# The final norm written with features on partitions instead of token rows

## The chip, the cores and the metric

The kernel runs on one core of one Trainium2 chip, in one launch. The metric is the time of an execution on the device in microseconds (us), of which the median of three runs is given.

## The reference, cut to what matters

One layer of a hybrid decoder and a final norm, all in float32, for 512 prompt tokens and 8 sample tokens of 1024 features. A recurrent mixer comes first; the part around the change is the MLP and the final norm:

```
h2 = rmsnorm(x, norm2_g) * (1 + sc2) + sh2
ff = square(relu(h2 @ w_ff1)) @ w_ff2          # 1024 -> 4096 -> 1024
x  = x + g2 * ff                               # g2: one row for the prompt, one per sample
y  = x * rsqrt(mean(x * x over features) + 1e-6) * final_norm_g
```

The outputs are y for the prompt and for the samples, and the states of the mixer.

## The kernel before, in words

All tokens stand side by side in one axis of T = 520 (512 prompt, 8 samples), cut into two halves of HALF = 260. Activations lie with features on partitions: `self.x` is a list of 8 tiles of 128 features x 520 tokens, called features or feature blocks 0 to 7 here. A float32 product is made of three matmuls with operands split into a high and a low part (`_split_w`, L107: the high part by a ScalarE cast, the low part by a VectorE subtraction).

The MLP (`mlp`, L1351) goes in four quarters q of the 4096 hidden features. In each, the second matrix is multiplied by a Strassen-like scheme: for each pair m of output blocks (2m and 2m + 1) there are seven products, named by j, of 12 matmuls over 260 columns each (`product`, L1180). Each product accumulates in a PSUM bank that it shares with others of its pair, and after each, `added` (L1303) reads the bank and adds what belongs to x: by VectorE directly, or by a ScalarE copy (`snap`, L1212) and an accumulating DMA from POOL. The eight sample columns are collected in `zs` and added at the pair's end. The order of the products is written out in `plan` (L1028); the last quarter ends with (2,1), (2,2), (2,6), (2,7), (3,1), (2,4), (3,6), (3,2), (3,7), (2,5), (3,4), (2,3), (3,5), (3,3), where (m,j) is pair and product. For m = 2, block 4 is complete in its first half after (2,2), (2,4) completes the first half of block 5, (2,5) its second, and (2,3) the second half of block 4. For m = 3 (`added_last`, L1447), block 6's first half is complete after (3,2), block 7's after (3,4), and the second halves after (3,5) for block 7 and (3,3) for block 6.

The framework's planner orders each engine's instructions by a simulated timeline; `urgent` raises a priority, and `InOrder` (L53) fixes the written order on TensorE, ScalarE and VectorE. From (3,4)'s result on everything is in the written order.

The final norm before writes y in token rows. `final_pair` (L1419) transposes two feature blocks of half the tokens on TensorE against the identity, sums squares over them on ScalarE, and multiplies by the norm's weights on VectorE (`gbc`, a row loaded by L1400 and spread over all partitions) into `fx`, 4 x 128 token rows of 1024 features; the samples go to `fxs`. Blocks 6 and 7 come last: `last_transposes` (L1543) multiplies by a diagonal of the norm's weights instead, and `last_sums` (L1550) adds their squares on TensorE to those collected. `last_half` (L1521), behind (2,3), makes the roots of the first 256 tokens and writes their rows, the part behind (3,3) the rest; `row` (L1566) multiplies 128 rows by their roots, one scalar per partition, in a piece of 768 and one of 256 features, and sends each off. Rows leave in runs of 3072 and 1024 bytes.

Of the kernel before, what the change touches and what calls it, by code (L numbers as in the profile page):

```python
# [6 lines left out]
F32 = mybir.dt.float32  # L7
# [4 lines left out]
OP = mybir.AluOpType  # L12
# [5 lines left out]
NB = 8  # L18
# [23 lines left out]
NM = 9  # L42
T2 = T + NM + 3
# [36 lines left out]
class Kernel:  # L80
# [188 lines left out]
    def load_parameters(self):  # L269
# [4 lines left out]
        self.gcol = self.pm[:, 70:72]  # L274
# [905 lines left out]
    def product(self, q, m, j, ks):  # L1180
# [13 lines left out]
        for k in ks:  # L1194
# [7 lines left out]
            if (q, m, j, k) == (3, 2, 3, 2):  # L1202
                self.last_rows = [self.ppb.tile([128, 512], F32, name="pb"), self.ppt.tile([128, 512], F32, name="pt")]
                self.last_transposes(0, 0)
                self.last_transposes(0, 1)
# [97 lines left out]
    def added(self, q, m, j, ps, s):  # L1303
# [35 lines left out]
        if j == 3:  # L1339
# [3 lines left out]
            if q == 3:  # L1343
                eng = nc.gpsimd if far else nc.vector
                for t in (0, 1):
                    eng.tensor_tensor(zs[t], zs[t], self.modc(5, 2 * m + t)[:, 1:9], OP.mult)
                    eng.tensor_tensor(x[t][:, L:], x[t][:, L:], zs[t], OP.add)
# [46 lines left out]
    def final_open(self):  # L1394
        nc, sm = self.nc, self.consts
        self.fx = self.act.tile([128, NC, D], F32, tag="h", name="fx", bufs=2)
        t = self.act.tile([128, 4, D], F32, tag="h", name="fin", bufs=2)
        self.gbc, self.fxs, self.junk = t[:, 0], t[:NB, 1], t[:, 2].rearrange("p (n f) -> p n f", f=256)
        self.njunk = 0
        nc.sync.dma_start(self.gbc, self.i["final_norm_g"].partition_broadcast(128))  # L1400
        self.fss = sm.tile([128, NC + 1, 4], F32, name="fss")
        nc.vector.memset(self.fss, 1.0)
        self.fr = sm.tile([128, 8], F32, name="fr")
        self.part = t[:, 3, 256:264]

# [680 lines left out]
```

## Time and profile before

| | us |
|---|---|
| median of three runs | 1005.66 (1005.57 to 1006.06) |
| the profiled execution | 1004.99 |
| its span, first to last instruction | 1003.2 |
| TensorE busy | 984.8 |
| VectorE busy | 690.4 |
| ScalarE busy | 524.3 |
| GpSimd (POOL) busy | 135.9 |

The span is what the trace covers; 1.8 us of the execution lie around it. The granted TensorE clock is 0.999 of full speed over the span. In the profile PE is TensorE, PEld its weight loads, DVE VectorE, ACT ScalarE, POOL GpSimd, SP the engine that issues most transfers; a q behind an engine's name is its sequencer. Instructions made through `InOrder` all carry line 72, so there the tile names tell them apart: `ma` is x, `snap` a copied product or a square, `fin` the final norm's tile, `mm`, `ps`, `pt` and `pb` are PSUM banks. A float32 matmul that is not split by hand appears as two instructions. The rows below are whole lines of the trace's views.

### The profile page before, as it was taken

The page shows a single profiled execution, that of the slowest core. Times are in us where ns is not written, and L with a number is a line of the kernel's source. Part 1 is how long each engine was busy: PE and PEld are TensorE (multiplying, and loading weights), DVE is VectorE, ACT ScalarE, POOL GpSimd, SP SyncE. Part 2 cuts the span into 40 slices and gives each one's busy share as a digit, 9 for nine tenths or more (in the row PEclk, how much of TensorE's full clock was granted, in tenths as well). Part 3 has the DMA queues.
Part 4 walks back from the last instruction along what each step waited for, and adds up shares of the span by engine and source line. Part 5 has one row for each costly group of instructions (what it writes and reads, how often), then busy time and mean ns, then how long its engine had stood idle before and what let it go on. Part 6 is the DMA issues. An engine that isn't in the chain of part 4 may idle for free. (4 is left out here: it accounts for less than half of the span.)

```text
span 1003.2 us, 23199 instructions
## 1 busy us (share of the span) xinstructions
PE 984.8 (98%) x9644; PEld 955.0 (95%) x9644; DVE 690.4 (69%) x1359; ACT 524.3 (52%) x996; POOL 135.9 (14%) x247
## 2 busy tenths in 40 slices
PE   8999999999999999999999999999999999999997
PEld 6899999999989999989999999999999999999996
DVE  7795966676595667887535456767767766768785
ACT  5565645734653572475412234466556545646662
POOL 1300000000000101121000000022321331232050
PEclk9999999999999999999999999999999999999999
DMA  9663343243244336345557665222752472272142
GB/s 350 241 193 123 103 156 123 86 143 130 98 135 152 101 98 213 112 148 179 199 169 276 221 218 194 85 85 56 175 153 80 104 194 83 64 189 65 64 85 86
DMA packets 48857, 143.67 MB, mean 143 GB/s; under 512 B 6240, under 2 KB 15904, under 8 KB 47720
## 3 DMA queue, kind: packets, MB, share of 16 engines
q1 hardware_dynamic: 37280, 123.47, 36.4%
q0 software_dynamic: 11456, 18.70, 8.3%
q8 instruction: 75, 1.23, 0.5%
q14 instruction: 30, 0.25, 0.1%
q10 hardware_dynamic: 16, 0.03, 0.0%
HBM read 123.65 MB, written 11.26 MB: 134 GB/s over the span
## 5 line engine op out<-in xcount | busy, mean ns | idle before, releaser
L155 PE MATMUL mm<-h,whi 128*128 128x260 f32 (+1 forms) x2720 | 451.4, 285 | 0.0
L155 PEld LDWEIGHTS mm<-h,whi 128*128 128x128 f32 x2720 | 378.3, 188 | 1.3 <-issue 0.6
L155 PE MATMUL mm<-h,wlo 128*128 128x260 f32 x1360 | 279.9, 285 | 2.6 <-DVE wlo L116 2.6
L116 DVE TENSOR_TENSOR wlo<-wst,whi 128x1024 fp32r<-128x1024 f32 x156 | 190.7, 1224 | 126.0 <-ACT whi L113 121.8
L113 ACT CAST whi<-wst 128x1024 fp32r<-128x1024 f32 x156 | 163.8, 1052 | 187.8 <-PE mm L155 142.1
L155 PEld LDWEIGHTS mm<-h,wlo 128*128 128x128 f32 x1360 | 212.4, 189 | 3.9 <-DVE wlo L116 3.2
L1293 POOL TENSOR_TENSOR ft<-ft,fsh 128x8 f32<-128x8 f32 x28 | 18.4, 659 | 209.2 <-DVE ft L1287 209.2
L1301 DVE TENSOR_TENSOR f<-f 128x260 f32<-128x260 f32 x64 | 27.3, 427 | 28.0 <-ACT f L1296 27.5
L1290 ACT ACTIVATE ft<-ft,fsh 128x512 f32<-128x512 f32 (+2 forms) x36 | 24.1, 677 | 36.0 <-DVE ft L1287 36.0
L155 PE MATMUL mm<-b,whi 128*128 128x260 f32 x256 | 41.6, 284 | 0.0
L155 PE MATMUL mm<-oa,whi 128*128 128x260 f32 x256 | 41.6, 284 | 0.0
L155 PE MATMUL mm<-a,whi 128*128 128x260 f32 x256 | 41.4, 284 | 0.0
L582 DVE TENSOR_TENSOR X<-X,tb 128x512 f32<-128x512 f32 x48 | 31.0, 690 | 12.5 <-PE ps L574 9.2
L155 PEld LDWEIGHTS mm<-oa,whi 128*128 128x128 f32 x256 | 34.8, 188 | 2.1 <-ACT whi L113 1.6
L155 PEld LDWEIGHTS mm<-b,whi 128*128 128x128 f32 x256 | 35.1, 188 | 1.7 <-ACT whi L113 1.2
L155 PEld LDWEIGHTS mm<-a,whi 128*128 128x128 f32 x256 | 35.0, 188 | 1.2 <-PE pt L359 0.8
L231 POOL TENSOR_SCALAR ss<-ss 128x4 f32<-128x4 f32 x8 | 2.7, 334 | 238.2 <-ACT g L666 238.1
L179 ACT ACTIVATE gate<-pb,pa 128x260 f32<-128x260 f32 x32 | 15.5, 485 | 31.1 <-PE pb L714 31.1
L1335 POOL DMA_DIRECT2D ma<-snap x28 | 26.2, 951 | 40.5 <-issue 28.7
L1317 POOL DMA_DIRECT2D ma<-snap x28 | 26.0, 929 | 37.8 <-DMA ma<-snap 22.4
L1296 ACT ACTIVATE f<-ft 128x520 f32<-128x520 f32 (+1 forms) x36 | 20.8, 589 | 15.1 <-POOL ft L1294 13.1
L155 PE MATMUL mm<-b,wlo 128*128 128x260 f32 x128 | 25.8, 283 | 0.0
(566 smaller groups left out, 2072.7 us busy)
## 6 DMA issues: line engine op xcount, KB each, us to landing
wst<-in_w_ff_dram SPq DMA_DIRECT2D x64, 512.0 KB, 4.1
wst<-in_w_in_dram SPq DMA_DIRECT2D x56, 512.0 KB, 3.7
wst<-in_w_mod_dram SPq DMA_DIRECT2D x32, 512.0 KB, 4.3
wm<-in_w_piece_dram SPq DMA_DIRECT2D x4, 1024.0 KB
wm<-in_w_rows_dram SPq DMA_DIRECT2D x4, 1024.0 KB, 12.1
st<-in_state_hgrn_dram SPq DMA_DIRECT2D x8, 512.0 KB, 3.8
vb<-vd SPq DMA_DIRECT2D x8, 512.0 KB, 4.0
out_dram<-st SPq DMA_DIRECT2D x8, 512.0 KB
```

Source lines behind the costliest of these rows:

```text
L113: ins = self.nc.scalar.copy(hi, st)
L116: self.nc.vector.tensor_tensor(lo, st, hi.bitcast(F32), OP.subtract)
L155: self.last_product = self.nc.tensor.matmul(ps[s][:, :c.stop - c.start], x, y[:, c], start=first and n == 0, stop=last and n == 2)
L179: ins = self.nc.scalar.activation(out, x, AF.Sigmoid, **kw)
L231: p.tensor_scalar(out, x, n * EPS, None, OP.add)
L582: last = nc.vector.tensor_tensor(half, half, factors(tbs, x, b), OP.mult)
L1290: nc.scalar.activation(t[:, :p], t[:, :p], AF.Relu, bias=sh[:, 0:1])
L1293: eng.tensor_tensor(t[:, p:], t[:, p:], sh[:, 1:9], OP.add)
L1296: nc.scalar.activation(f, self.two(self.ft)[:, a:a + n], AF.Square)
L1301: self.nc.vector.tensor_tensor(f[:, n], f[:, a], f[:, b], op)
L1317: nc.gpsimd.dma_start(x[1][:, b], v[:, :n], accum_op=OP.add)
L1335: nc.gpsimd.dma_start(x[t][:, a], s[p], accum_op=OP.add)
```

## The change

The result stays with features on partitions. Its output is one array of 8 x 128 x 520, features by tokens, which is only laid out anew outside the kernel. No block of x is transposed any more and the row of norm weights isn't loaded.

For each block, `final_in` squares it on ScalarE, makes `xg`, the block times the norm's weights (one scalar per partition, `gcol`), by a ScalarE Copy, and adds the square to `total` on VectorE. When a half of all blocks is in, `final_roots` sums `total` over partitions on TensorE, in three groups of 87 tokens (matmuls of one column with `total` as weights), and takes the root on ScalarE; `final_diagonals` inverts it and makes three 87 x 87 diagonals on VectorE; `final_spread` multiplies them by ones, so that a PSUM bank holds each token's factor on all partitions; and `final_out` multiplies blocks a to b of half s by that bank on VectorE and sends them off, in runs of 260 tokens (1040 bytes). The first half's sums and diagonals come behind (2,3), its spread behind (3,5); all multiplies come behind (3,3), where block 6's second half takes weights and factor in one instruction. The sample columns of the odd blocks are now finished after j = 5, those of the even ones after j = 3.

```diff
--- before.py
+++ after.py
@@ -40,6 +40,7 @@
 
 
 NM = 9
+GROUP = 87
 T2 = T + NM + 3
 PAIR = "pair"
 EARLY = 8
@@ -271,7 +272,7 @@
         self.pm = self.consts.tile([128, 72], F32, name="pm")
         self.nc.sync.dma_start(self.pm, self.i["params_mod"])
         self.bmod, self.n1g, self.n2g = self.pm[:, 0:48], self.pm[:, 48:56], self.pm[:, 56:64]
-        self.gcol = self.pm[:, 70:72]
+        self.gcol = self.pm[:, 64:72]
         self.pl = self.start.tile([128, 16], F32, name="pl")
         self.nc.sync.dma_start(self.pl, self.i["params_bound"])
         self.pa = t = self.hc.tile([128, 313], F32, name="pa")
@@ -1199,10 +1200,6 @@
                                             stop=k == 3 and n == 2, skip_group_check=True)
                 self.behind(ins, self.last_product)
                 self.last_product = ins
-            if (q, m, j, k) == (3, 2, 3, 2):
-                self.last_rows = [self.ppb.tile([128, 512], F32, name="pb"), self.ppt.tile([128, 512], F32, name="pt")]
-                self.last_transposes(0, 0)
-                self.last_transposes(0, 1)
         if ks[-1] == 3:
             if (q, m) == (3, 3):
                 self.added_last(j, ps)
@@ -1340,11 +1337,10 @@
             with self.urgent():
                 nc.vector.scalar_tensor_tensor(x[0][:, b], ps[:, :n], g[0], x[0][:, b], OP.mult, OP.add)
                 nc.vector.tensor_tensor(zs[0], zs[0], ps[:, n:], OP.add)
-            if q == 3:
-                eng = nc.gpsimd if far else nc.vector
-                for t in (0, 1):
-                    eng.tensor_tensor(zs[t], zs[t], self.modc(5, 2 * m + t)[:, 1:9], OP.mult)
-                    eng.tensor_tensor(x[t][:, L:], x[t][:, L:], zs[t], OP.add)
+        if q == 3 and j in (5, 3):
+            t, eng = int(j == 5), nc.gpsimd if far else nc.vector
+            eng.tensor_tensor(zs[t], zs[t], self.modc(5, 2 * m + t)[:, 1:9], OP.mult)
+            eng.tensor_tensor(x[t][:, L:], x[t][:, L:], zs[t], OP.add)
         if q == 3:
             self.final_after(m, j)
 
@@ -1392,57 +1388,79 @@
         self.load()
 
     def final_open(self):
-        nc, sm = self.nc, self.consts
-        self.fx = self.act.tile([128, NC, D], F32, tag="h", name="fx", bufs=2)
-        t = self.act.tile([128, 4, D], F32, tag="h", name="fin", bufs=2)
-        self.gbc, self.fxs, self.junk = t[:, 0], t[:NB, 1], t[:, 2].rearrange("p (n f) -> p n f", f=256)
-        self.njunk = 0
-        nc.sync.dma_start(self.gbc, self.i["final_norm_g"].partition_broadcast(128))
-        self.fss = sm.tile([128, NC + 1, 4], F32, name="fss")
-        nc.vector.memset(self.fss, 1.0)
-        self.fr = sm.tile([128, 8], F32, name="fr")
-        self.part = t[:, 3, 256:264]
-
-        self.gdiag = t[:, 3, :256].rearrange("p (j f) -> p j f", j=2)
-        self.one, self.summed = self.ones_r.bitcast(F32)[:, 0:1], set()
+        t = self.act.tile([128, KO * T2], F32, tag="h", name="xg", bufs=2)
+        self.xg = t[:, :KO * T].rearrange("p (s m n) -> p s m n", s=2, m=KO)
+        t = self.act.tile([128, KO, T2], F32, tag="h", name="fin", bufs=2)
+        self.total, self.fsq, self.nsq = t[:, 0, :T], [t[:, 1 + n, :T] for n in range(5)], 0
+        self.diag = [t[:GROUP, 6 + s, :3 * GROUP].rearrange("p (i n) -> p i n", i=3) for s in range(2)]
+        self.fr = self.consts.tile([128, 8], F32, name="fr")
+
+    def final_in(self, t, *halves):
+
+        nc, x = self.nc, self.x[t]
+        c = slice(halves[0] * HALF, (halves[-1] + 1) * HALF)
+        if t:
+            self.nsq = (self.nsq + 1) % 5
+        sq = (self.fsq[self.nsq] if t else self.total)[:, c]
+        nc.scalar.activation(sq, x[:, c], AF.Square)
+        if (t, halves) != (6, (1,)):
+            nc.scalar.activation(self.xg[:, halves[0]:halves[-1] + 1, t], self.two(x)[:, halves[0]:halves[-1] + 1], AF.Copy,
+                                 scale=self.gcol[:, t:t + 1])
+        if t:
+            return lambda: nc.vector.tensor_tensor(self.total[:, c], self.total[:, c], sq, OP.add)
 
     def final_after(self, m, j):
         if (m, j) in ((2, 2), (2, 7)):
-            self.final_pair(int(j == 7), 0)
-            self.final_pair(int(j == 7), 1)
-        if (m, j) == (2, 7):
-            for t in range(2):
-                self.nc.vector.tensor_scalar(self.gdiag[:, t], self.ident, self.gcol[:, t:t + 1], None, OP.mult)
+            for t in (0, 1) if j == 2 else (2, 3):
+                add = self.final_in(t, 0, 1)
+                if add:
+                    add()
+        if (m, j) == (2, 4):
+            for t in (4, 5):
+                self.final_in(t, 0)()
+        if (m, j) == (2, 5):
+            self.final_in(5, 1)()
         if (m, j) == (2, 3):
-            self.last_half()
-
...
+            with self.urgent():
+                self.fsum, self.frs = (self.pmm.tile([128, 2, 512], F32, name="mm") for _ in range(2))
+                add = self.final_in(4, 1)
+                self.final_roots(0)
+                add()
+                self.final_diagonals(0)
+
+    def final_groups(self, s):
+        return [s * HALF + c for c in (0, GROUP, HALF - GROUP)]
+
+    def final_sums(self, s):
+        for n, c in enumerate(self.final_groups(s)):
+            self.nc.tensor.matmul(self.fsum[:GROUP, s, n:n + 1], self.total[:, c:c + GROUP],
+                                  self.ones_r.bitcast(F32)[:, 0:1], start=True, stop=True)
+
+    def final_roots(self, s):
+        self.final_sums(s)
+        r = self.fr[:GROUP, 4 * s:4 * s + 3]
+        self.nc.scalar.activation(r, self.fsum[:GROUP, s, :3], AF.Sqrt, bias=self.epsc[:GROUP], scale=1.0 / D)
+
+    def final_diagonals(self, s):
+        r = self.fr[:GROUP, 4 * s:4 * s + 3]
+        self.nc.vector.reciprocal(r, r)
+        self.nc.vector.tensor_tensor(self.diag[s], self.ident[:GROUP, None, :GROUP].to_broadcast([GROUP, 3, GROUP]),
+                                     r[:, :, None].to_broadcast([GROUP, 3, GROUP]), OP.mult)
+
+    def final_spread(self, s):
+        for n, c in enumerate(self.final_groups(0)):
+            self.nc.tensor.matmul(self.frs[:, s, c:c + GROUP], self.ones_r.bitcast(F32)[:GROUP], self.diag[s][:, n],
+                                  start=True, stop=True)
+
+    def final_out(self, s, a, b):
+
+        y, r = self.xg[:, s, a:b], self.frs[:, s, :HALF]
+        if (s, a) == (1, 6):
+            self.nc.vector.scalar_tensor_tensor(y[:, 0], self.x[6][:, HALF:], self.gcol[:, 6:7], r, OP.mult, OP.mult)
+        else:
+            self.nc.vector.tensor_tensor(y, y, r[:, None].to_broadcast([128, b - a, HALF]), OP.mult)
+        queue = self.nc.scalar if (s, a) in ((1, 4), (0, 6)) else self.nc.sync
+        queue.dma_start(self.o["y"][a:b, :, s * HALF:(s + 1) * HALF].rearrange("m p t -> p m t"), y)
 
     def added_last(self, j, ps):
         n = L - HALF
@@ -1458,121 +1476,53 @@
         def add_samples(t, op=OP.add):
             self.nc.vector.tensor_tensor(zs[t], zs[t], ps[:, n:], op)
 
-        def samples_done(eng, t):
+        def samples_done(t):
+            eng = self.nc.gpsimd
             eng.tensor_tensor(zs[t], zs[t], self.modc(5, 6 + t)[:, 1:9], OP.mult)
             eng.tensor_tensor(x[t][:, L:], x[t][:, L:], zs[t], OP.add)
 
         with self.urgent():
             if j == 1 or j == 2:
                 add(0, g[0])
+            if j == 2:
+                self.final_in(6, 0)()
             if j == 6:
                 add(1, ng)
-                self.final_pair(2, 0)
             if j == 7:
                 add(1, g[1], True)
                 add_samples(1)
             if j == 4:
+                self.nc = InOrder(self.tc)
                 add(1, g[1])
-                self.nc, self.squares = InOrder(self.tc), {}
-                self.last_parts(0)
-                self.last_squares(0, 0)
-                self.last_squares(0, 1)
+                self.final_in(7, 0)()
             if j == 5:
                 add(1, ng, True)
-                add(0, g[0], True)
                 add_samples(1, OP.subtract)
-                add_samples(0)
-                samples_done(self.nc.gpsimd, 1)
-                self.last_squares(1, 1)
-            if j == 3:
-                self.last_rows = [self.pmm.tile([128, 2, 512], F32, name="mm")[:, 0],
-                                  self.pps.tile([128, 512], F32, name="ps")]
-                self.last_transposes(1, 1)
-                self.last_sums(1, 1)
+                samples_done(1)
                 add(0, g[0], True)
                 add_samples(0)
-                samples_done(self.nc.vector, 0)
-                self.last_squares(1, 0)
-                self.last_sums(1, 0)
-                self.last_transposes(1, 0)
...
+                samples_done(0)
+                self.final_in(7, 1)()
+                self.final_spread(0)
+            if j == 3:
+                nc = self.nc
+                add(0, g[0], True)
+                t = self.sm.tile([128, NB], F32, name="rst")
+                nc.vector.tensor_tensor(t, ps[:, n:], self.modc(5, 6)[:, 1:9], OP.mult)
+                nc.vector.tensor_tensor(x[0][:, L:], x[0][:, L:], t, OP.add)
+                last = self.final_in(6, 1)
+                self.final_out(0, 0, 2)
+                last()
+                self.final_roots(1)
+                self.final_out(0, 2, 4)
+                self.final_diagonals(1)
+                self.final_out(0, 4, 6)
+                self.final_spread(1)
+                self.final_out(1, 0, 4)
+                self.final_out(1, 4, 6)
+                self.final_out(1, 6, 7)
+                self.final_out(1, 7, 8)
+                self.final_out(0, 6, 8)
 
     def run(self):
         tc, i, enter = self.tc, self.i, self.ctx.enter_context
@@ -2013,7 +1963,7 @@
 
 
 _OUTS = [
-    ("y_p", (1, 512, 1024)), ("y_s", (8, 1, 1024)), ("hgrn_p", (1, 1, 8, 128, 128)), ("hgrn_s", (8, 128, 1024)),
+    ("y", (8, 128, 520)), ("hgrn_p", (1, 1, 8, 128, 128)), ("hgrn_s", (8, 128, 1024)),
     ("xlast", (128, 88)), ("hlast", (128, 72)), ("conv_old", (8, 2, 1024)),
 ]
 
...
@@ -2082,4 +2031,5 @@
     xlast, hlast = rows(o["xlast"], 11), rows(o["hlast"], 9)
     hgrn_s = o["hgrn_s"].reshape(H, 128, NB, 128).transpose(2, 0, 1, 3)[None]
     conv_s = np.concatenate([o["conv_old"], xlast[3:, None]], 1)[None]
-    return (o["y_p"], o["y_s"], o["hgrn_p"], hlast[None, :1], xlast[None, None, :3], hgrn_s, hlast[None, 1:], conv_s)
+    y = np.ascontiguousarray(o["y"].transpose(2, 0, 1)).reshape(T, D)
+    return (y[None, :L], y[L:, None], o["hgrn_p"], hlast[None, :1], xlast[None, None, :3], hgrn_s, hlast[None, 1:], conv_s)
```

## Rows read from the trace of the kernel before

**Rows 1.** The chain that ended last, in order of time: start us, us, what.

```profile
998.21 0.40 DVEq L2069
```

**Rows 2.** Busy time by stretch: us, busy per engine (instructions), clock, DMA share, GB/s.

```profile
965.00:985.40 20.40, 20.40 (x174) 20.31 (x173) 16.64 (x32) 11.21 (x33) 5.04 (x9) 1.00 0.09 14
985.40:992.50 7.10, 7.10 (x62) 6.87 (x60) 3.31 (x13) 3.29 (x10) 0.00 (x0) 1.00 0.22 87
992.50:998.70 6.20, 3.17 (x29) 2.72 (x28) 5.08 (x19) 2.53 (x6) 0.41 (x2) 1.00 0.34 129
```

**Rows 3.** Timeline of TensorE and weight loads: start us, us, engine, line, instruction.

```profile
946.53 0.28 PE L1198 MATMUL ps<-ff0h,xhi 128*128 128x260 f32 x1
...
985.42 0.28 PE L72 MATMUL ps<-ff0h,whi 128*128 128x260 f32 x1
...
987.64 0.31 PEld L72 LDWEIGHTS mm<-fin,ident 128*128 128x128 f32 x2
...
988.68 0.67 PEld L72 LDWEIGHTS mm<-ident,ma 128*128 128x128 f32 x6
...
989.37 0.19 PEld L72 LDWEIGHTS ps<-ff0h,whi 128*128 128x128 f32 x1
...
990.92 0.28 PE L72 MATMUL ps<-ff0h,whi 128*128 128x260 f32 x1
...
992.24 0.28 PE L72 MATMUL ps<-ff3h,wlo 128*128 128x260 f32 x1
```

**Rows 4.** Tile ma, 940 to 1000: count, min/median/max ns, first to last.

```profile
L1432 PE MATMUL mm<-ident,ma x20: 270/273/273, 964.0 to 982.3; 128*128 128x128 f32 x20
...
L1435 PE MATMUL mm<-ident,ma x4: 270/272/273, 970.7 to 976.2; 128*8 128x128 f32 x4
```

**Rows 5.** Timeline of VectorE and ScalarE around product (2,3).

```profile
985.62 0.49 DVE L1456 SCALAR_TENSOR_TENSOR ma<-pt,modT,ma 128x260 f32<-128x260 f32 x1
...
986.14 0.42 ACT L72 ACTIVATE snap<-ma 128x256 f32<-128x256 f32 x1 [1.29 <-DVE ma L1456]
...
987.95 0.48 DVE L72 SCALAR_TENSOR_TENSOR ma<-ps,modT,ma 128x252 f32<-128x252 f32 x1 [1.85 <-PE ps L72]
...
988.96 0.26 ACT L72 ACTIVATE fr<-mm,epsc 128x2 f32<-128x2 f32 x1 [2.40 <-PE mm L72]
```

**Rows 6.** VectorE's groups by shape, 946.4 to 992.4: count, busy us, mean ns, idle.

```profile
L1442 DVE TENSOR_TENSOR fx<-mm,fin 128x512 f32<-128x512 f32 x5 | 3.4, 679 | 1.2 <-ACT fin L1437 1.2
...
L1337 DVE TENSOR_TENSOR ma<-ma,snap 128x260 f32<-128x260 f32 x2 | 0.8, 420 | 0.0
```

**Rows 7.** ScalarE's groups by shape, 946.4 to 992.4.

```profile
L1437 ACT ACTIVATE fin<-mm 128x256 f32<-128x256 f32 x10 | 3.9, 387 | 6.2 <-PE mm L1432 4.6 <-PE mm L1435 1.4
L1227 ACT CAST ff3h<-f 128x260 fp32r<-128x260 f32 x6 | 2.1, 409 | 0.4 <-DVE f L1301 0.4
L1437 ACT ACTIVATION_READ_ACCUMULATOR fin<-mm 128x1 f32 x10 | 2.0, 196 | 0.0
...
L1145 ACT CAST xhi<-wst 128x512 fp32r<-128x512 f32 x2 | 1.3, 632 | 0.0
```

**Rows 8.** Timeline of VectorE behind the last product.

```profile
994.12 0.48 DVE L72 SCALAR_TENSOR_TENSOR ma<-ps,modT,ma 128x252 f32<-128x252 f32 x1
...
994.90 0.17 DVE L72 TENSOR_TENSOR ma<-ma,zs 128x8 f32<-128x8 f32 x1
```

**Rows 9.** Timeline of SP: the first and the last issue of output rows.

```profile
990.11 0.34 SPq L1575 DMA_DIRECT2D out_dram<-fx  x1
...
998.68 0.59 SPq L1575 DMA_DIRECT2D out_dram<-fx  x1
```

**Rows 10.** Busy time by short stretch, for the DMA share and GB/s.

```profile
990.60:991.00 0.40, 0.40 (x5) 0.40 (x5) 0.00 (x0) 0.40 (x3) 0.00 (x0) 1.00 0.13 54
...
993.20:993.40 0.20, 0.00 (x0) 0.00 (x0) 0.20 (x2) 0.00 (x0) 0.00 (x0) 1.00 0.98 338
...
1001.20:1001.60 0.40, 0.00 (x0) 0.00 (x0) 0.00 (x0) 0.00 (x0) 0.00 (x0) 0.50 0.03 10
```

More of the change, by code (lines that the diff above doesn't have):

```diff
@@ L1521, in last_half @@
-    def last_half(self):
-        with self.urgent():
-            self.sums = self.pmm.tile([128, 2, 512], F32, name="mm")
-            self.last_sums(0, 0)
-            self.last_sums(0, 1)
-            self.last_root(self.fr[:, :2], self.sums[:, 0, :2])
-            self.row(0, self.nc.scalar)
-            self.row(1, self.nc.vector)
-            self.row(0, self.nc.scalar, self.last_rows[0])
-            self.row(1, self.nc.vector, self.last_rows[1])
-            self.final_pair(2, 1)
-            self.last_parts(1)
@@ L1535, in last_parts @@
-    def last_parts(self, s):
-        ts = slice(2 * s, NC + 1 if s else 2)
-        self.nc.vector.tensor_reduce(self.part[:, ts], self.fss[:, ts, :3], mybir.AxisListType.X, OP.add)
-    def last_squares(self, s, j):
-        self.squares[s, j] = self.misc.tile([128, HALF], F32, name="snap", bufs=7)
-        self.nc.scalar.activation(self.squares[s, j][:, :256], self.x[6 + j][:, 256 * s:256 * s + 256], AF.Square)
-    def last_transposes(self, s, j):
-        for t in range(2):
-            c = (2 * s + t) * 128
-            self.nc.tensor.matmul(self.last_rows[t][:, j * 128:(j + 1) * 128], self.x[6 + j][:, c:c + 128],
-                                  self.gdiag[:, j], start=True, stop=True)
@@ L1550, in last_sums @@
-    def last_sums(self, s, j):
-        ps = self.sums[:, s, :2]
-        first = (s, 1 - j) not in self.summed
-        self.summed.add((s, j))
-        if first:
-            self.nc.tensor.matmul(ps, self.ident, self.part[:, 2 * s:2 * s + 2], start=True, stop=True,
-                                  skip_group_check=True)
-        for t in range(2):
-            self.nc.tensor.matmul(ps[:, t:t + 1], self.squares[s, j][:, t * 128:(t + 1) * 128], self.one, start=False,
-                                  stop=True, skip_group_check=True)
@@ L1562, in last_root @@
-    def last_root(self, r, ss):
-        self.nc.scalar.activation(r, ss, AF.Sqrt, bias=self.epsc[:r.shape[0]], scale=1.0 / D)
-        self.nc.vector.reciprocal(r, r)
-    def row(self, t, eng, p=None):
-        c = slice(0, 768) if p is None else slice(768, D)
-        y, r = self.fx[:, t, c], self.fr[:, t:t + 1]
-        src = y if p is None else p[:, :256]
-        if eng is self.nc.scalar:
-            eng.activation(y, src, AF.Copy, scale=r)
-        else:
-            eng.tensor_scalar(y, src, r, None, OP.mult)
-        self.nc.sync.dma_start(self.o["y_p"][0, t * 128:(t + 1) * 128, c], y)
+                samples_done(0)
@@ L2052, in layouts @@
         "state_conv": i["state_conv"],
-        "final_norm_g": i["final_norm_g"],
     }
```

45 lines of the change are left out of this document (removed).

## The prediction

> **What bounds the kernel now.** I read the page for the span, then the chain of waits, then busy time by stretch, and last the order of instructions on each engine from 946 us on, because everything that the diff touches runs there. The chain [rows 1] is short: it goes back only through the last roots and row multiplies, and its last piece ends at 998.6. Behind it stand only output transfers, and the span ends at 1003.2. Busy time by stretch [rows 2] shows two regimes. From 946.5 to 992.5 TensorE is busy all the time, while VectorE has 16.64 of 20.40 us and ScalarE 11.21 in the second stretch. After 992.5 TensorE is at half and VectorE at 5.08 of 6.20. So a TensorE instruction taken out before 992.5 moves the end directly, as long as VectorE and ScalarE follow; behind that the serial chain and the transfers count.
>
> How full TensorE is can be checked: a product's 12 matmuls start 0.12 us apart (990.92 to 992.24 is 11 steps [rows 3]), so 1.44 us a product. 28 products of the last quarter are 40.3 us. The stretch from 946.53 to 992.36 takes 45.8. The missing 5.5 us is the normalization's own TensorE work: 30 transposes (24 in [rows 4], 6 from 988.68 to 989.37) at 0.69 / 6 = 0.115 us make 3.45; the transposed first half of features 6 and 7, 8 instructions inside (2,3), takes 0.90 (985.42 to 987.64 less 11 steps), and the sums of the first half, 10 instructions, 1.04 (987.64 to 988.68) [rows 3]. That is 5.4: practically no stall is in the stretch.
>
> **The change, part by part.** I call A the start of product (2,3), 985.42 before [rows 3], and R the moment when VectorE can read the last product, (3,3). (2,3)'s last matmul starts with the next group's weight load at 987.64, and VectorE reads it at 987.95 [rows 3, 5]: 0.31 later. So R was 992.24 + 0.31 = 992.55. VectorE came to it only at 994.12 [rows 8]: it was 1.6 us late with the pair of features 4 and 5 that was normalized in between.
>
> *Up to A.* The 24 transposes of [rows 4] go: 24 x 0.115 = -2.76 us. What must keep pace is VectorE and ScalarE. VectorE loses five multiplies of 0.679 and two of 256 columns at about 0.41, some 4.2 us. It gains the total's adds: three of 520 columns at about 0.69 (by the line through 0.420 for 260 and 0.679 for 512 columns [rows 6]), four of 260 at 0.42, and two small sample operations, 4.1 us. ScalarE loses 10 squares of 0.387 with their accumulator reads of 0.196 and two more such pairs, 7 us, and gains a Square and a scaled Copy of four whole features at about 0.64 (0.632 for 512 columns) and of four halves at 0.409, 8.4 us [rows 7]. The sums fit: VectorE has 16.5 us to do in 17.6 where it had 16.64 in 20.40, and since its rows overlap by some 0.07 each, really about 14.3. It is full but not over. I take all of the 2.76; the ends are -2.76 and 0 (VectorE or ScalarE becomes the bound and TensorE waits out what it saved). The 512 KB load of the final norm's weights goes too; no product reads it and the weight loads behind it wait for VectorE anyway, so I cost it at nothing (if it did hold them up, its going is a gain). On POOL the sample work of features 0 and 2 keeps its place and that of 1 and 3 moves from j = 3 up to j = 5; nothing waits there.
>
> *From A to R.* TensorE's order is now (2,3), three sums, (3,5), three spreads, (3,3). Without stalls: 3 x 1.44 + 6 x 0.104 (10 sum instructions took 1.04) + 6 x 0.113 (8 instructions of 128 columns took 0.90 [rows 3]) + 0.19 to R = 5.8 us. But both insertions hang on chains that now run serially. The sums need feature 7's first half: its add starts at A + 0.20 [rows 3, 5], or up to 0.37 later behind the sample operations of feature 5; I take A + 0.37, 0.49 for the add, Square 0.42 [rows 5], total add 0.42, with 0.03 for each hand-over: A + 1.76. (2,3) is over at A + 1.44, so TensorE stands 0.3. Sums to 2.4, (3,5) to 3.9. The spreads need the root: VectorE's four operations behind (2,3) take 0.95 (as 994.12 to 995.07 [rows 8]), then on ScalarE Square 0.42, Copy 0.42 and the Sqrt 0.26 [rows 5], all in the written order, then a reciprocal of 0.17 and the diagonals of 261 columns, 0.42: A + 4.45. TensorE stands 0.6, spreads to 5.18, (3,3) to 6.62, R at A + 6.81, against 7.13 before: -0.32. The ends are 5.8 (everything ready) and 7.9 (another 1.1 of queueing on ScalarE, whose Copies stand in the order ahead of the Sqrt). Behind the waiting spreads only (3,3) is queued, and that is the path.
>
> *From R to the last byte.* Before: R 992.55, last issue 998.68 [rows 9], packets until about 1001.2 [rows 10]: 8.65 us. Now VectorE is free at R: add 0.39 and two small ones 0.37 (0.95 with one more [rows 8]). Then Square 0.42 beside the first multiply (520 columns, 0.69), total add to R + 1.73, three sums 0.62 + 0.2 to 2.55, Sqrt to 2.85, reciprocal and diagonals to 3.5 (each after a multiply that VectorE does in the meantime), spreads 0.68 + 0.2 to 4.4, the four-block multiply of 1040 columns, 1.22 by the line of [rows 6], to 5.65. Its transfer is issued at 5.68; packets follow 0.84 after an issue (990.11, and 990.95 where the share sets in [rows 9, 10]), R + 6.5. The multiplies end at 7.6, with 0.61, 0.4, 0.35 and 0.61 for the last four; but the 10 blocks issued from 5.68 on are 1280 packets of 1040 bytes, 80 for each of 16 engines, and the engines are the limit. 1024-byte packets ran at 338 GB/s at a share of 0.98 [rows 10], 47.5 ns each; 1040 bytes then take 48.2, all 3.9 us. The trace of before has no such short runs at odd addresses going out, so the other end is a quarter more, 4.9. I take 4.2, near the row: R + 10.7, which is +2.05. Reading half the multiplies from PSUM changes nothing: the 0.679 row reads PSUM as well. From the last packet to the span's end stay 2.0 us [rows 1, 10].
>
> The Trainium skill, "DMA: Bandwidth & Descriptors", section "How a descriptor splits into AXI transactions", says that a descriptor which doesn't start on a 256-byte boundary pays for the bytes between the boundary below and its start. The blocks here start at multiples of 1040, so on average 120 bytes would be wasted, an estimate of 54 ns a packet and 4.3 us for the 80; the sum below would be -0.9 by it, and -1.3 by the row's 48.2 ns. The rows here can't show it.
>
> *Sum:* -2.76 - 0.32 + 2.05 = -1.03 us. The profiled execution took 1004.99 (span 1003.2 and 1.8 around it), 0.67 under the median of the runs shown, 1005.66. So 1003.96 for such an execution, 1004.6 us for the median. 0.2% is 2.0 us, about what a measurement of this kernel tells from no change: this forecast is inside it.
>
> **Rivals.**
> *No stalls:* the planner puts adds and Squares early enough, R comes at A + 5.8 and packets take 48 ns: -1.0 and -0.3 more, 1003.3; the range's low end leaves 0.7 more, for a first four-block transfer that starts earlier than my chain of ten hand-overs says. For it: VectorE is idle 1.85 us ahead of 987.95 [rows 5]. Against: the written order puts Copies ahead of the Sqrt.
> *The saving turns into waiting (slower):* TensorE runs up against VectorE and ScalarE between 965 and A. A product that accumulates into a bank waits for the copy out of the one two places before, some 1.44 us of slack; Squares and Copies of 0.641 stand in ScalarE's queue ahead of such copies, and if one waits for a feature's last accumulation, the casts behind it wait too. From 1.44 us of delay on TensorE stalls; if it takes all of the 2.76, the time is 1004.6 + 2.8 = 1007.4. For it: 16.64 of 20.40 [rows 2]. Against: the work removed equals the work added.
> *Slow writes:* runs of 1040 bytes at twice the time, 95 ns: 7.6 instead of 4.2 us, 1008.0. For it: nothing in the trace shows such writes. Against: 1024-byte runs go at almost the full rate.
>
> **How the numbers follow.** Forecast with its own range 1003.7 to 1006: 0.6 (stalls and packets between their ends, part of the 2.76 lost). No stalls: 0.22. Waiting: 0.12, half of it past 1007. Slow writes: 0.06. Likeliest 1004.6; the range goes to 1002.6 and 1007.2. Faster by over 0.2% (below 1003.65) takes the no-stall case and the forecast's edge, 0.27; slower (above 1007.7) half of the two bad ones, 0.09; the same, 0.64.
>
> **What would show it.** (2,3) starting near 982.7 shows the first step; gaps of 0.3 and 0.6 us ahead of sums and spreads the second; R + 5.65 for the four-block multiply's end and a share near 1 for 4 us the third. A gap ahead of a product between 965 and A, or a share of 1 for over 5.5 us, makes it wrong.

## The result and the profile after

| | before | after |
|---|---|---|
| median, side by side on one chip | 1005.62 us (6 runs, 1004.36 to 1006.72) | 1009.16 us (6 runs, 1007.71 to 1009.99) |
| profiled execution, span | 1004.99, 1003.2 | 1009.06, 1007.3 |

The ratio is 1.0036 (95% interval 1.0026 to 1.0046): the changed kernel is 3.5 us slower. The forecast was 1004.6, inside 0.2% of no change. It is wrong, and the time lies above its range.

In the kernel after, instructions made through `InOrder` carry line 73, a product's matmuls L1199, ScalarE's copies out of a bank L1217, the Squares L1405 and the Copies into `xg` L1407. First TensorE's timeline (start us, us, engine, line, instruction; in brackets the idle time ahead of it and what ended it), the rows that answer to [rows 3]:

```profile
966.38 0.36 PE L1199 MATMUL ps<-ff0h,xhi 128*128 128x260 f32 x1 [0.35 <-DVE zs L1339]
...
969.22 0.28 PE L1199 MATMUL pb<-ff3h,wlo 128*128 128x260 f32 x1
971.58 0.39 PE L1199 MATMUL ps<-ff0h,whi 128*128 128x260 f32 x1 [2.08 <-ACT snap L1217]
...
973.15 0.42 PE L1199 MATMUL pt<-ff0h,whi 128*128 128x260 f32 x1
...
975.75 0.42 PE L1199 MATMUL ps<-ff0h,xhi 128*128 128x260 f32 x1
...
977.54 0.28 PE L1199 MATMUL pt<-ff0h,whi 128*128 128x260 f32 x1
...
986.18 0.28 PE L73 MATMUL ps<-ff0h,whi 128*128 128x260 f32 x1
987.90 0.62 PE L73 MATMUL mm<-ones_r,fin 128*87 128x1 f32 x6
...
990.70 0.90 PE L73 MATMUL mm<-fin,ones_r 87*128 87x87 f32 x6 [0.62 <-DVE fin L73]
991.39 0.37 PE L73 MATMUL ps<-ff0h,whi 128*128 128x260 f32 x1
994.94 0.62 PE L73 MATMUL mm<-ones_r,fin 128*87 128x1 f32 x6 [1.86 <-DVE fin L73]
997.18 1.58 PE L73 MATMUL mm<-fin,ones_r 87*128 87x87 f32 x6 [1.62 <-DVE xg L73]
```

The second and third rows are the largest loss. Product (2,2) issues its last matmul at 969.22, and (2,6), which should follow 0.12 later, starts at 971.58: TensorE stood until ScalarE had copied product (2,1) out of the bank that (2,6) writes. The next rows are starts of (2,7), (3,1) and (2,4): 1.57, 2.60 and 1.79 us apart, where a product takes 1.44. Busy time by stretch says why; behind PE, PEld, DVE, ACT and POOL stand the granted clock, the DMA share and GB/s:

```profile
972.00:973.00 1.00, 1.00 (x10) 1.00 (x9) 1.00 (x3) 0.68 (x2) 0.00 (x0) 1.00 0.00 0
973.00:974.00 1.00, 1.00 (x7) 1.00 (x6) 0.89 (x2) 0.56 (x2) 0.00 (x0) 0.54 0.00 0
974.00:975.00 1.00, 1.00 (x6) 1.00 (x6) 0.12 (x1) 0.85 (x1) 0.00 (x0) 0.50 0.00 0
...
976.00:977.00 1.00, 1.00 (x8) 1.00 (x8) 0.39 (x2) 1.00 (x3) 0.00 (x0) 0.75 0.00 0
977.00:978.00 1.00, 1.00 (x10) 1.00 (x10) 0.41 (x2) 0.09 (x1) 0.00 (x0) 1.00 0.00 0
996.00:997.00 1.00, 0.00 (x0) 0.00 (x0) 0.97 (x3) 0.00 (x0) 0.00 (x0) 0.99 0.83 284
997.00:998.00 1.00, 0.81 (x4) 0.82 (x5) 0.13 (x1) 0.00 (x0) 0.00 (x0) 0.50 0.26 93
...
1000.00:1001.00 1.00, 0.00 (x0) 0.00 (x0) 1.00 (x4) 0.00 (x0) 0.00 (x0) 0.50 0.02 6
1001.00:1002.00 1.00, 0.00 (x0) 0.00 (x0) 0.98 (x3) 0.00 (x0) 0.00 (x0) 0.50 0.98 329
1002.00:1003.00 1.00, 0.00 (x0) 0.00 (x0) 0.00 (x0) 0.00 (x0) 0.00 (x0) 0.50 1.03 359
1003.00:1004.00 1.00, 0.00 (x0) 0.00 (x0) 0.00 (x0) 0.00 (x0) 0.00 (x0) 0.50 1.02 338
1004.00:1005.00 1.00, 0.00 (x0) 0.00 (x0) 0.00 (x0) 0.00 (x0) 0.00 (x0) 0.50 0.89 300
```

In [rows 2] the clock was 1.00 in all of this stretch. Now it is at half (1.2 of 2.4 GHz) from 973.0 on, 1.4 us after TensorE had taken up work again, and back in the course of 976 to 977. At the end it halves once more, at 997, where TensorE had stood 1.86 and 1.62 us. The last four rows are the output transfers, near the full share: with the 0.02 of the row ahead of them their shares make 3.94 us. Why the copy was late is in ScalarE's timeline:

```profile
965.16 1.99 ACT L114 CAST whi<-wst 128x1024 fp32r<-128x1024 f32 x2
968.14 1.17 ACT L1405 ACTIVATE fin<-ma 128x520 f32<-128x520 f32 x2 [0.98 <-DMA ma<-snap]
969.22 1.95 ACT L1407 ACTIVATE xg<-ma,pm 128x520 f32<-128x520 f32 x3
971.08 0.45 ACT L1217 ACTIVATE snap<-ps,modT 128x260 f32<-128x260 f32 x1
```

(2,1) was complete at about 968.1 (its 12 matmuls start from 966.38 on). In ScalarE's queue two Squares and three Copies stood ahead of its copy, and the first Square waited 0.98 us for an accumulating DMA into its block. The copy ran at 971.08, three microseconds late; (2,2) covered part of it. The first row of TensorE's timeline is another stand: (2,1) starts 0.49 us late, because VectorE reads its bank (L1338, L1339) only behind weight work:

```profile
963.96 1.21 DVE L117 TENSOR_TENSOR wlo<-wst,whi 128x1024 fp32r<-128x1024 f32 x1
965.09 0.69 DVE L1159 TENSOR_TENSOR wst<-wst 128x512 f32<-128x512 f32 x1
965.70 0.47 DVE L1338 SCALAR_TENSOR_TENSOR ma<-ps,modT,ma 128x252 f32<-128x252 f32 x1
966.09 0.15 DVE L1339 TENSOR_TENSOR zs<-zs,ps 128x8 f32<-128x8 f32 x1
```

The end, on VectorE:

```profile
993.11 0.48 DVE L73 SCALAR_TENSOR_TENSOR ma<-ps,modT,ma 128x252 f32<-128x252 f32 x1 [0.54 <-PE ps L73]
...
996.10 0.43 DVE L73 TENSOR_TENSOR fin<-ident,fr 87x261 f32<-87x261 f32 x1
996.45 0.69 DVE L73 TENSOR_TENSOR xg<-xg,mm 128x520 f32<-128x520 f32 x1
998.80 1.84 DVE L73 TENSOR_TENSOR xg<-xg,mm 128x1040 f32<-128x1040 f32 x2 [1.67 <-PE mm L73]
```

R is the first row here, 993.11: VectorE now comes to (3,3) as soon as it can read it, where the same instruction before, the first of [rows 8], was 1.6 us late. The diagonals of half 1 are done at 996.53, but the spread starts only when the multiply of blocks 4 and 5 ends (997.14), and takes 1.58 us instead of the 0.90 of half 0's. VectorE stands 1.67 us for it.

The account, with S for the start of the stretch (product (0,1) of the last quarter, 946.53 before [rows 3], 945.69 after):

| us | before | forecast | after |
|---|---|---|---|
| S to A | 38.89 | 36.13 | 40.49 |
| A to R | 7.13 | 6.81 | 6.93 |
| R to the last packet | 8.65 | 10.7 | 11.8 |
| last packet to the span's end | 2.0 | 2.0 | 2.4 |

S itself isn't counted: it lies between 945.40 and 947.58 in the thirteen traces, whatever the kernel. So what the going of the 512 KB load is worth, which the prediction took as nothing, can't be read from these traces.

### The profile page after: what moved, and what is told of

It is laid out like the page before. It is cut to its first block, busy times and chain, and to the rows that moved or that the text cites. A ratio compares the mean times of both kernels' runs of the same rounds, so it can differ in the third digit from the quotient of the medians.

```text
span 1007.3 us, 23067 instructions
## 1 busy us (share of the span) xinstructions
PE 982.0 (97%) x9592; PEld 951.8 (94%) x9592; DVE 692.6 (69%) x1356; ACT 523.3 (52%) x980; POOL 136.8 (14%) x249
## 5 line engine op out<-in xcount | busy, mean ns | idle before, releaser
L156 PE MATMUL mm<-a,wlo 128*128 128x260 f32 x128 | 25.8, 283 | 0.0
```

The costliest lines, as they stand in the source:

```text
L156: self.last_product = self.nc.tensor.matmul(ps[s][:, :c.stop - c.start], x, y[:, c], start=first and n == 0, stop=last and n == 2)
```

## The experiments

Each was timed beside the kernel before on the same chip. The theory: what the kernel loses against the forecast comes from (a) the stand ahead of (2,6), by the order of ScalarE's queue, (b) the halved clock behind it, (c) the late and slow spread of half 1. Rivals: VectorE and ScalarE have too much work in the stretch, whatever their order; the transfers set the end.

| run | ratio to before (95%) | S to A | A to the span's end |
|---|---|---|---|
| before | | 38.89 | 17.78 |
| after | 1.0036 (1.0026 to 1.0046) | 40.49 | 21.12 |
| e1_copy_first | 1.0014 (1.0004 to 1.0024) | 37.86 | 20.94 |
| e2_xg_later | 1.0006 (0.9997 to 1.0016) | 36.93 | 20.69 |
| e3_fill_gap | 1.0027 (1.0018 to 1.0036) | 39.05 | 20.35 |
| e5_spread_early | 1.0020 (1.0011 to 1.0030) | 38.30 | 20.96 |
| e4_tail_warm | 1.0019 (1.0010 to 1.0028) | 40.65 | 20.3 |
| e7_three | 1.0004 (0.9995 to 1.0013) | 36.92 | 20.25 |
| e8_order | 0.9996 (0.9987 to 1.0004) | 36.94 | 19.85 |
| e9_order_cold | 1.0002 (0.9993 to 1.0011) | 36.95 | 20.47 |
| e10_own_bank | 0.9983 (0.9975 to 0.9992) | 36.92 | 18.73 |
| e11_bank_alone | 1.0029 (1.0019 to 1.0039) | 40.34 | 20.38 |
| e12_first_early | 0.9986 (0.9977 to 0.9994) | 36.93 | 19.10 |

The last two columns are of each kernel's one profiled execution; the span's end is known to 0.1 us. The kernels "after", e4, e5 and e11 have the same text up to A, so their spread in the third column (38.30 to 40.65) is one between executions.

**e1_copy_first and e2_xg_later: the order of ScalarE's queue.** Squares and Copies of blocks 0 to 3 are ordered behind the copy of (2,1) in e1, the Copies alone in e2. The edit of e2, cut; e1 does the same with the Square's instruction too:

```diff
         if j == 1:
             s[1] = self.snap(ps, g[0])
+            if (q, m) == (3, 2):
+                self.hold = self.last_copy
...
+            ins = nc.scalar.activation(self.xg[:, halves[0]:halves[-1] + 1, t], self.two(x)[:, halves[0]:halves[-1] + 1], AF.Copy,
                                  scale=self.gcol[:, t:t + 1])
+            if t < 4:
+                self.behind(ins, self.hold)
```

> The changed kernel with one ordering edge: on ScalarE the Squares and Copies of features 0 to 3 stand behind the copy of product (2,1). Theory: in the changed kernel TensorE stood 2.1 us ahead of (2,6) (971.58) because that copy lay behind three Squares and three Copies in ScalarE's queue, one of them waiting 1.0 us for an accumulating DMA, and the stand then brought the granted clock to half for 3.3 us (16 matmuls 0.217 instead of 0.12 us apart, 1.5 us). Without it: (2,6) follows (2,2) with no gap, clock 1.00 throughout, (2,3) starts near 982.4 instead of 986.2, time 1009.2 - 3.7 = 1005.5 us. Rival: ScalarE is simply too full there; the wait moves on to the next copy, of (2,6) or (2,7), or to a weight cast, and the time falls by 1 us at most, to 1008.

> Only the Copies of features 0 to 3 (the multiplications by the norm's weights) stand behind the copy of (2,1); the Squares stay ahead of it, with their wait for the DMA. Theory: the copy of (2,1) starts at 969.3 instead of 971.08, (2,6) waits 0.5 us instead of 2.1, too short to lose the clock: 1009.2 - 1.8 - 1.5 = 1005.9 us. Rival on the clock: any stand of TensorE here costs the clock, then -1.8 alone, 1007.4. Rival of a full ScalarE: 1008.

ScalarE in e2 (Squares here L1407, Copies L1409):

```profile
967.26 1.17 ACT L1407 ACTIVATE fin<-ma 128x520 f32<-128x520 f32 x2 [0.31 <-POOL ma L1345]
968.34 0.46 ACT L1217 ACTIVATE snap<-ps,modT 128x260 f32<-128x260 f32 x1
968.70 1.96 ACT L1409 ACTIVATE xg<-ma,pm 128x520 f32<-128x520 f32 x3
```

The copy runs at 968.34 instead of 971.08, (2,6) starts at 969.13 without a gap (the expected half microsecond did not come, as the Squares' wait was 0.31 instead of 0.98), and S to A is 36.93: 1.96 of the 2.76 us are gained. In e1 (2,6) has no gap either, but the Squares, moved too, push a weight cast and two later copies back: (2,4) starts 0.6 us late and (3,6) loses 0.5; A is 0.9 later than in e2. (The text on e1 counts three Squares ahead of the copy; two stand behind the wait, one ran before it.) By their ratios e2 is 3.0 us faster than the changed kernel, where 3.3 were expected, and e1 2.2, between its theory (3.7) and its rival (1 at most): there part of the wait did move on. In both the clock stays at 1.00 up to A. So the same work fits into the stretch but for 0.8 us: the loss was the order, and "too much work" falls.

**e3_fill_gap: meant to show the clock by itself.** 20 extra matmuls, read by nobody, stand ahead of (2,6).

```diff
+        if (q, m, j) == (3, 2, 6):
+            fill = self.pmm.tile([128, 2, 512], F32, name="mm")[:, 0, :HALF]
+            for _ in range(20):
+                ins = self.nc.tensor.matmul(fill, hi[:, 0], self.ff[0][0][:, 0], start=True, stop=True)
```

> The changed kernel with 20 extra matmuls of 260 columns between (2,2) and (2,6), into a PSUM bank that nobody reads: 2.4 us of TensorE work in the place of the stand. Theory: the stand itself stays (the copy of (2,1) is as late as before), but TensorE is never idle, the clock stays at 1.00, and the 1.5 us that 16 matmuls at half rate cost come back: 1009.2 - 1.5 + 0.2 = 1007.9 us. Rival: the half rate has another cause than the stand: the time is the same or 0.3 us longer, 1009.4.

TensorE's timeline, the extra matmuls and the starts of (2,6) and (2,7), then ScalarE's Squares and the copy of (2,1):

```profile
969.05 2.56 PE L1198 MATMUL mm<-ff0h,whi 128*128 128x260 f32 x20
971.45 0.28 PE L1205 MATMUL ps<-ff0h,whi 128*128 128x260 f32 x1
...
972.89 0.28 PE L1205 MATMUL pt<-ff0h,whi 128*128 128x260 f32 x1
```

```profile
967.18 1.17 ACT L1411 ACTIVATE fin<-ma 128x520 f32<-128x520 f32 x2 [0.31 <-POOL ma L1349]
...
970.11 0.46 ACT L1223 ACTIVATE snap<-ps,modT 128x260 f32<-128x260 f32 x1
```

(2,6) starts at 971.45, the products behind it are 1.44 apart at a clock of 1.00, and S to A is 1.44 shorter than in the changed kernel. This looks like part (b) by itself, but the execution doesn't show it. Here the Squares waited 0.31 us instead of 0.98, and the copy of (2,1) ran at 970.11; (2,6) follows that copy's start by 0.50 in the changed kernel and in e5, so it could have started at 970.61. It was the 20 matmuls that held it until 971.45. Without them the stand would have been that of e5 below, and there the clock stayed at 1.00 with nothing filled in. The time is open too: 0.9 us under the changed kernel relative to before, as expected, but the two intervals overlap.

**e5_spread_early: the spread of half 1 ahead of the multiply of blocks 4 and 5.**

```diff
-                self.final_out(0, 4, 6)
                 self.final_spread(1)
+                self.final_out(0, 4, 6)
```

> In the tail the spread of the second half's roots stands, in the written order, ahead of the multiply of the first half's blocks 4 and 5 instead of behind it. Theory: the spread waited until 997.18 for that multiply though its diagonals were ready at 996.53; it now starts 0.6 us earlier and with it everything behind: 1009.2 - 0.6 = 1008.6 us. VectorE's order changes little: the multiply runs while TensorE spreads. Rival: the wait was for the diagonals with a longer hand-over, nothing changes, 1009.2.

The spread now starts right behind the diagonals, 1.64 us after the sums instead of 2.24, as expected. But it gains nothing: the multiply of blocks 4 and 5 now waits for the spread in its turn, and the four-block multiply starts 3.87 us after the sums, where it was 3.86. By its ratio the run is 1.6 us faster than the changed kernel all the same, though the two intervals overlap a little. Its profiled execution lost less ahead of A, where the edit changes nothing:

```profile
970.96 0.39 PE L1199 MATMUL ps<-ff0h,whi 128*128 128x260 f32 x1 [1.41 <-ACT snap L1217]
...
972.51 0.28 PE L1199 MATMUL pt<-ff0h,whi 128*128 128x260 f32 x1
```

Here the stand was 1.41 instead of 2.08, and no slow clock followed: (2,7) comes 1.55 after (2,6), the clock is 1.00 from 972 to 977. With the same text up to A, e4 and e11 stood 2.22 and 1.91 us there and lost the clock as the changed kernel did: in each of the three traces the three products from (2,6) on took 1.6 us longer than three products at the full clock. So the same text has both forms, and single profiles differ by some 2 us. This is the evidence for (b): the clock halved behind the three longer stands, not behind the shorter one, and not in the seven runs whose order edit left no stand there.

**e4_tail_warm: the clock at the end.** 14 extra matmuls ahead of the sums of half 1 and 8 behind them.

```diff
+                fill(14)
                 last = self.final_in(6, 1)
                 self.final_out(0, 0, 2)
...
                 self.final_roots(1)
+                fill(8)
```

> Matmuls whose result nobody reads are put ahead of the sums of half 1 (14) and between these sums and the spread (8); all else is the changed kernel. Theory: the spread of half 1 takes 1.58 us because TensorE stood and its clock is at half from 997 us on; kept busy, it takes some 0.85, and the four-block multiply and all behind it come 0.7 us earlier: about 1008.5 against 1009.2 for the changed kernel on the same scale. Rival: the end does not hang on the spread's length (the transfers of the other blocks fill the time), or the extra matmuls delay the sums: 1009.2 or a little more.

```profile
997.69 0.90 PE L73 MATMUL mm<-fin,ones_r 87*128 87x87 f32 x6 [0.55 <-DVE xg L73]
```

The spread takes 0.90 instead of 1.58, and the four-block multiply starts 3.18 us after the sums instead of 3.86: the 0.7 expected. All five traces with these extra matmuls (e4, e7, e8, e10, e12) have a spread of 0.90. Of the seven without them, five have 1.58, but e2 has 1.26 and e3, behind the same stands, 0.90:

```profile
995.51 0.90 PE L73 MATMUL mm<-fin,ones_r 87*128 87x87 f32 x6 [1.62 <-DVE xg L73]
```

So the clock's fall comes at slightly different times from one execution to the next, and most of the 0.8 us by which e3 is shorter than the changed kernel behind A is this. Relative to the kernel before, e4's time is 1.7 us under that of the changed kernel, more than expected; with intervals of 0.9 us each way it can't be told whether the rest is chance.

**e7_three, e8_order, e9_order_cold: the edits together, and the order of the multiplies.** e7 is e2, e5 and e4 at once. e8 also moves a multiply and splits one (its edit against e7, cut, is shown); e9 is e8 without the extra matmuls.

```diff
                 self.final_out(0, 4, 6)
-                self.final_out(1, 0, 4)
+                self.final_out(0, 6, 8)
+                self.final_out(1, 0, 2)
+                self.final_out(1, 2, 4)
                 self.final_out(1, 4, 6)
...
-                self.final_out(0, 6, 8)
```

> Three edits at once: the Copies of features 0 to 3 behind the copy out of the bank that holds product (2,1), the spread of half 1 ahead of the multiply of blocks 4 and 5, and the extra matmuls at the end. Theory: their gains lie in different places and add up, 1006.2 - 0.6 - 0.7 = 1004.9, which is the time that the prediction gave (1004.6) but for the part of the transposes' 2.76 us that is still lost. Rival: the edits at the end bring nothing, since the transfers of 80 packets an engine set it: 1006.2.

> The three edits, and the order of the last multiplies: blocks 6 and 7 of half 0 right behind blocks 4 and 5 instead of last, and blocks 0 to 3 of half 1 in two pieces of two blocks. Theory: VectorE stands 1.67 us ahead of the four-block multiply in the changed kernel, so the moved multiply costs nothing, its 16 packets an engine leave the last burst (16 x 49 ns = 0.8 us), and the first transfer of half 1 is released 0.6 us earlier: 1004.9 - 1.4 = 1003.5, faster than the kernel before by 2 us. Rival: the moved multiply (0.7 us) now delays the multiplies of half 1 by as much as the burst becomes shorter: 1004.9.

> As the run before it but without the extra matmuls at the end. Theory: the spread of half 1 is again 0.7 us longer; VectorE has 1.4 us of multiplies of half 0 to do meanwhile, and so at most 0.7 shows: between 1003.5 and 1004.2. Rival: the half clock delays everything behind it as in the changed kernel: 1004.2 or more.

Relative to the kernel before, all three came out above the theory: by 1.1 us (e7), 1.7 (e8) and at least 1.6 (e9); e7 is hardly faster than e2. One row of VectorE in e8 shows what is in the way:

```profile
993.99 3.12 DVE L73 TENSOR_TENSOR xg<-xg,mm 128x520 f32<-128x520 f32 x5 [0.99 <-PE mm L73]
```

The five multiplies begin with two of half 0, whose factors had been there since 988, yet VectorE stood 0.99 us until half 1's spread was over. Both spreads lie in one PSUM tile, `frs`, and the wait goes by the tile, as e10 and e11 show. That is why in the changed kernel the spread waited for the multiply, and why turning their order round only turned the wait round. In e7 and e8 the multiplies held back also send their transfers in the last burst; its share in e8:

```profile
995.00:996.00 1.00, 0.00 (x0) 0.00 (x0) 1.00 (x3) 0.00 (x0) 0.00 (x0) 1.00 0.34 120
996.00:997.00 1.00, 0.00 (x0) 0.00 (x0) 1.00 (x2) 0.00 (x0) 0.00 (x0) 0.98 1.04 340
...
1000.00:1001.00 1.00, 0.00 (x0) 0.00 (x0) 0.00 (x0) 0.00 (x0) 0.00 (x0) 0.50 0.31 109
```

With 1.04, 1.02 and 1.02 in between it is 4.77 us for 96 packets an engine, where the changed kernel had 80. e9, with the clock low in the spread (1.58 us), ends 0.6 later behind A than e8: the moved multiplies don't hide it, since they wait for it.

**e10_own_bank, e11_bank_alone, e12_first_early: a PSUM tile of its own for half 1's spread.** e10 is e8 with it, e11 the changed kernel with it alone. e12 is e10 with the first multiply ahead of VectorE's last addition. The edit of e11, cut; in e10 the tile is the one that the extra matmuls write (`self.frs1 = warm`).

```diff
+            r = self.frs1 if s else self.frs[:, 0]
+            self.nc.tensor.matmul(r[:, c:c + GROUP], self.ones_r.bitcast(F32)[:GROUP], self.diag[s][:, n],
                                   start=True, stop=True)
...
-        y, r = self.xg[:, s, a:b], self.frs[:, s, :HALF]
+        y, r = self.xg[:, s, a:b], (self.frs1 if s else self.frs[:, 0, :HALF])
...
+                self.frs1 = self.ppb.tile([128, 512], F32, name="pb")[:, :HALF]
                 self.final_spread(1)
```

> As the run with the three edits and the new order of the multiplies (e8_order, 0.3 us under the kernel before), with one more edit: the spread of half 1 goes to a PSUM tile of its own instead of the second part of the tile that holds half 0's. Theory: the multiplies of half 0 need nothing of half 1's spread, yet VectorE stood 0.99 us until it ended, because both halves lie in one tile; with two tiles VectorE begins right behind the diagonals, everything behind comes 1.0 us earlier, and the time is 1.3 us under the kernel before. Rival: the transfers set the end (96 packets an engine follow one another from the first one on, whatever VectorE does): no more than 0.3 under it.

> The changed kernel with nothing but the PSUM tile of its own for half 1's spread. Theory: the wait of the spread for the multiply of blocks 4 and 5 (0.62 us) goes and nothing else changes: about 3.0 us above the kernel before, where the changed kernel is 3.6 above it. Rival: the spread waits for the written order on another engine, not for the tile: 3.6.

> As e10_own_bank, and the first multiply (blocks 0 and 1 of half 0) stands ahead of VectorE's last addition of a product, where VectorE stood 0.54 us. Theory: the multiplies behind the diagonals of half 1 become one fewer (0.6 us), so the first transfer of half 1 is released 0.6 us earlier and the last burst is 80 packets an engine instead of 96: 1.9 us under the kernel before. Rival: the multiply (0.69 us) does not fit into the 0.54 us, or is late itself, and delays the last addition and all behind it: 1.2 under it or less.

VectorE in e10, from the diagonals on:

```profile
994.19 0.43 DVE L73 TENSOR_TENSOR fin<-ident,fr 87x261 f32<-87x261 f32 x1
994.54 1.29 DVE L73 TENSOR_TENSOR xg<-xg,mm 128x520 f32<-128x520 f32 x2
995.75 1.90 DVE L73 TENSOR_TENSOR xg<-xg,pb 128x520 f32<-128x520 f32 x3
```

The wait is gone: the multiplies of half 0 follow the diagonals at once, those of half 1 follow them, and A to the span's end is 18.73 against 19.85 in e8, the 1.1 us that the wait was worth. The kernel is faster than before by 0.17% (0.08 to 0.25%), 1.7 us where 1.3 were expected, so it is faster than both kernels, and the rival (transfers alone set the end, 0.3 at most) falls. In e11 the spread starts 1.64 us after the sums instead of 2.24, with nothing else changed:

```profile
998.31 1.58 PE L73 MATMUL pb<-fin,ones_r 87*128 87x87 f32 x6 [1.01 <-DVE fin L73]
```

By the trace the tile was the cause of the 0.6; the time (2.9 us above before, expected 3.0, rival 3.6) can't tell them apart. e12's time, 1.4 us under the kernel before (0.6 to 2.3), decides neither for the 1.9 expected nor for its rival's 1.2. By the trace the theory failed: A to the span's end is 19.10, no shorter than the 18.73 of e10. The last addition came no later, but the slot in which the first multiply had run was left empty (VectorE waits there for ScalarE's Square), so two multiplies still stood behind the diagonals.

## Why the prediction was wrong

*Up to A: "I take all of the 2.76".* This step failed: S to A grew by 1.60 us instead of falling by 2.76, a miss of 4.36. The products show where: (2,1) comes 0.49 late, (2,6) 2.24, and the three behind it lose 0.13, 1.16 and 0.35 to the clock. The argument was a sum of VectorE's and ScalarE's work over 20 us. The sum held, as e2 shows: with the same instructions in another order, 1.96 of the 2.76 came, with VectorE busy 15.60 and ScalarE 11.98 us of the 18.46 up to A. (Its last step was a misreading, though: the busy time in [rows 2] counts overlapping rows once already, as the durations of the 32 instructions add up to 19.15 us and not to 16.64; so the 16.5 can't be lowered to 14.3.) But a sum over a stretch says nothing of a queue in which a copy that TensorE needs at 968.1 stands behind 3.1 us of work that nobody needs before 988, with a wait for a DMA at its head.

*The rival was the right one.* "The saving turns into waiting" named this mechanism (Squares and Copies ahead of the copy out of a bank, one of them waiting for an accumulation) and nearly its size: the stands make 2.73 of the 2.76, 2.24 by that mechanism and 0.49 by VectorE's late read. The sign that the prediction named, a gap ahead of a product between 965 and A, came. The rival was given 0.12, because "the work removed equals the work added", which is not evidence against an order. And it had no price for the clock: 1.64 us more.

*From A to R* the working held: the sums came at A + 1.72 (said 1.76), behind a gap of 0.28 (0.3); the spread at A + 4.52 (4.45) behind 0.62 (0.6); R at A + 6.93 (6.81).

*From R to the last packet.* Up to the diagonals it held (R + 3.42, said 3.5). Then the spread waited for a multiply through the shared tile (0.6, e11) and ran at the half clock (0.7, e4); the four-block multiply ended at R + 6.93 instead of 5.65, and that is the 1.1 us of the table but for a burst that was shorter than said. The sentence "each after a multiply that VectorE does in the meantime" saw the multiplies, and not that one of them locks the spread's tile.

*Slow writes* fell: 3.94 us for 80 packets an engine is 49.3 ns each, near the first end of the range (48.2, from [rows 10]), and not the 52 of the likeliest value or 95; e8 gives 49.7. A packet of 1040 bytes takes 47 ns by its own record (the median), one of 1024 bytes in the kernel before 46. The Trainium skill, "DMA: Bandwidth & Descriptors", section "How a descriptor splits into AXI transactions", by which the estimate was 54 ns, is not borne out to that amount here.

*What e2 doesn't recover* is 0.80 us of the 2.76, and nearly all of it is waiting for VectorE: (2,1) is 0.49 late in e2 as in the changed kernel, by the read shown above, and (3,6) loses 0.27 at its third matmul, which starts 0.05 behind the weight part (`wlo`) that it multiplies by:

```profile
974.07 1.22 DVE L117 TENSOR_TENSOR wlo<-wst,whi 128x1024 fp32r<-128x1024 f32 x1
975.34 0.39 PE L1199 MATMUL ps<-ff0h,wlo 128*128 128x260 f32 x1
```

In the kernel before TensorE had four transposes (967.39 to 967.74) to do ahead of (2,1).

*Still open:* why the Squares wait 0.3 us in some executions (e2, e3, e5, for POOL's sample addition) and 0.8 to 1.1 in others (the changed kernel and e4 for the DMA, e11 for POOL), which makes the stand 1.41 or some 2 us. And that the stand itself, and not something that comes with it, halves the clock ahead of (2,4) is argued from which executions show both; no trace has a long stand filled.

## What to carry to other kernels

Where removed work is replaced by as much other work, compare orders and not sums: for each engine that feeds the busy one, ask what stands in its queue ahead of the instruction that the busy engine waits for, and what that waits for. Work that is only needed later belongs behind such an instruction by an explicit order (one ordering edge, worth 3 us here). Two halves of a computation that are to overlap need tiles of their own: here a PSUM tile shared by both made the one wait for the other in whichever order they were written.

## What the runs showed of the hardware

A stand of 2.08 us on a TensorE that had been busy at the full clock was followed by 3.4 us at half of it, which began 1.4 us after work was taken up again. Behind stands of 2.22 and 1.91 us in the same place (e4, e11) the clock was 0.50 and 0.53 from 974 to 976; behind one of 1.41 us (e5) it stayed at 1.00. So a stand can cost nearly twice its length (2.24 and 1.64 here).

At the end, extra matmuls in the stands kept the clock at 1.00 through the spread in five traces of five; without them it had fallen by then in five of seven, in a sixth it fell within the spread, and in e3 it held. Not every fall belongs to the change: the traces of e10 and e11 also have 3.4 us at half the clock around 452 to 456 us.

1040-byte runs that start at multiples of 1040 bytes left at 49.3 and 49.7 ns a packet and engine, near the 47.5 of the 1024-byte runs in the kernel before.
